# A two-layer hybrid inference step on one core: the instruction order of all engines found with a timeline model as the scheduler's clock

## The chip, the core and the metric

The kernel runs on one core of one Trainium2 chip. The metric is the device time of one launch in microseconds (us). Five engines work side by side, each on a queue of its own that it takes in order: PE (matrix products; PEld is its weight load, which overlaps), DVE and POOL (elementwise work), ACT (activations and copies) and SP (which here only issues DMAs). They wait for one another by semaphores that the framework places. All of the program is unrolled: one stream of instructions per engine, 34,294 in all, with no loop left at run time. So the order in each stream is fixed when the program is built, and it is what this change is about.

## What is computed

One step of a decoder trunk with two layers, for 528 prompt tokens (16 of them learned) and 8 sample sequences of 4 tokens, which carry states; 560 tokens of 1024 features in all. Cut to the frame:

```python
def _trunk(x, states, p, n_lead):
    for l in range(DEPTH):                     # DEPTH = 2
        if l % 2 == 0:
            mix, s_g, s_r, s_sh = _ab_mixer(...)   # GLA and RWKV-7 behind one input projection
        else:
            mix, c_buf, s_d = _c_mixer(...)        # gated DeltaNet, chunks, triangular solve
        x = _layer_norm(DEEPNORM_ALPHA * x + mix, ...)
        f, f_buf = _conv_ffn(x, ...)               # W_down(silu(conv3(x W_gate)) * (x W_up)), D_FF = 2816
        x = _layer_norm(DEEPNORM_ALPHA * x + f, ...)
```

All is float32 for the reader. The recurrences (RWKV-7, GLA, DeltaNet) carry a state per head from one tile of tokens to the next.

## The kernel before

**Products.** Each weight tile of 128 output features comes from memory as float32 (`wraw`, three buffers, fetched by SP at L117/118) and is split into a high part `wh` (ACT, L95) and a low part `wl` (DVE or POOL, L96). A product is three matmuls, high by high, high by low and low by high (`accum`, L145 to L150, the matmul at L148). One tile of a projection (`proj_h`, L157) is two halves of the tokens by eight tiles of 128 inputs by three, 48 matmuls, into a PSUM bank called `ph`.

**Layer 0** (`ab_layer`, L1772). First the RWKV projections that the first two pairs of heads need. Then core 0 (two pairs of heads: the recurrence) while the next projection tiles run beside it; what is then left of the projections; then core 1 (the other two pairs) while the GLA core runs beside it; then the output projection with residual and layer norm (`out_proj`), and the feed-forward block `ffn`, whose down projection ends in a layer norm as well. **Layer 1** (`c_layer`, L1836) is the same in kind: the inputs of four heads, core 0 beside the inputs of the other four, core 1 beside the gates and the finish of the first four, then output projection, norm, feed-forward and the last norm, which writes y.

**A core** goes through five tiles of tokens, the last of which holds the sample tokens. For each there is `prep` (L895 in RWKV, L1560 in DeltaNet): products of keys, a triangular inverse in up to six levels (`tri_inverse`, L684), a solve (`tri_solve`, L745). Then `step` (L976, L1656): the state's way through the tile, with the state update `pS` at L1009/L1010 (RWKV) and L1677 (DeltaNet). There are two sets of buffers, taken by the parity of the tile, so prep of tile i+2 waits for step of tile i. In an inverse level PE (`px`, `pt`, `pw`) and DVE (`X`, sums) take turns; nothing in one level can start before the one ahead of it is done. After the fifth tile the sample sequences' states are updated (`sample_states`, L1049 and L1717). The sample tokens' reads of their own states are `psr` (L272).

**What sets the order.** Python code traces all instructions, and each gets a priority from the place of its trace: a lower number goes first. The context (`tile.TileContext`, opened in `kernel` at L1921) holds a scheduler that goes through time with a clock: at each moment, each engine takes the instruction with the lowest number among those whose operands it holds to be ready. `beside` and `tick` (L166 to L178) hand the scheduler work to fill in with: at each tick of a core some pieces of a generator are traced, with their priority raised by an offset, so that they count as later work:

```python
    def tick(self):
        self.credit += self.rate
        while self.side is not None and self.credit >= 1:
            self.credit -= 1
            tc.cur_priority = tc.cur_priority + self.off
            if next(self.side, self) is self:
                self.side = None
            tc.cur_priority = tc.cur_priority - self.off
```

The rates are pieces per tick (.35 in core 0 of layer 0, .3 in both cores of layer 1, a piece being a half of a projection tile), the offsets 1000 and 1500. They are the same before and after the change. The projection tiles so handed over are called filler below; the `ph` matmuls are nearly all of it.

**The layer norm** (`LN`, L412 to L545) works by halves of the tokens of 280 and 280. A half's last projection comes in eight tiles by pairs (`pd`). After the second pair, a first estimate of the mean is made: DVE sums (L475, L478), a matmul `pc` (L479), a copy (ACT L483) and four subtractions of it on DVE (L487); then squares (ACT L500) and sums (POOL L489 to L495, DVE L490 to L517), a matmul pair `pst` (L520), the inverse deviation (L527 to L531), and the norm itself on eight tiles (DVE L539 multiplies, L540 subtracts, ACT L541 scales). The first half's norm runs beside the second half's projection. In the last norm each tile is then written to y (L543).

Of the kernel before, what the change touches and what calls it, by code (L numbers as in the profile page):

```python
# [48 lines left out]
class K:  # L49
# [26 lines left out]
    @contextmanager  # L76
    def later(self):
        """What is traced here gives way to what is traced after it."""
        tc = self.tc
        p = tc.cur_priority  # L80
        tc.cur_priority = p + 1000000
        yield
        tc.cur_priority = p
# [20 lines left out]
    def ahead(self, src, k):  # L104
        """The next projection's weights, prepared before what is traced until then."""
        self.pre.append(self.prepared(src, k))
# [14 lines left out]
    def proj_n(self, pool, src, xh, xl, cols, evict, room=None):  # L121
        """A projection to 32 outputs: the products with either part of the weights on 32 partitions each."""
        w, _ = self.prepared(src, KT, room) if room else self.weights(src, KT)
        for c, m in cols:
            ps = pool.tile([128, 512], F32, tag="pj", name="ph")
            for i in range(KT):
                for x in (xh, xl):
                    self.nc.tensor.matmul(
                        ps[:64, :m], w[:, i], x[:, i, c : c + m], start=(i == 0 and x is xh), stop=(i == KT - 1 and x is xl)
                    )  # L130
            evict(slice(c, c + m), ps[:64, :m])
            yield
# [24 lines left out]
    def proj_h(self, pool, src, k, xh, xl, cols, evict):  # L157
        """A projection by halves of the tokens, one PSUM bank each: evict(half, result)."""
        w = self.weights(src, k)
        for c, m in cols:  # L160
            ps = pool.tile([128, 512], F32, tag="pj", name="ph")
            self.accum(ps, w, k, xh, xl, c, m)
            evict(slice(c, c + m), ps[:, :m])
            yield

    def beside(self, gen, rate, off=OFF):  # L166
        """What gen traces is traced beside what follows, rate of its pieces at each tick."""
        self.side, self.rate, self.credit, self.off = gen, rate, 0.0, off
# [11 lines left out]
    def rest(self, off=0):  # L180
        """The end of what runs beside."""
        if self.side is not None:
            self.tc.cur_priority = self.tc.cur_priority + off
            for _ in self.side:
                pass
            self.tc.cur_priority = self.tc.cur_priority - off
        self.side = None

    def norm(self, bank, room, pieces, terms, eps, use):
        """1 / sqrt of sums over the features of four heads (weights, what is summed), a quarter of the partitions  # L190
        each, and from there, in two parts on two partitions, to all partitions: use(head, columns, result)."""
# [29 lines left out]
    def log_exp(self, after):  # L221
        """The table set with both functions, loaded when what gives them their input has been issued."""
        if self.table:
            return None
        self.table = True
        i = self.nc.scalar.preload_act_table_set("natural_log_exp_and_others")
        self.behind(i, after)
        return i
# [28 lines left out]
def room_for_reads(k, pool, **a):  # L257
    """Where the sample tokens of a sequence have columns of their own, among zeros: [sequence, kind and token]."""
    z = pool.tile([128, 576], F32, name="zq", **a)
    k.nc.gpsimd.memset(z, 0.0)  # L260
    return z


def sample_reads(k, z, xs, load, ps):
    """Two kinds of columns of the sample tokens times their own sequences' states."""
    for n, x in enumerate(xs):
        own = z[:, 32 * n : 32 * n + 544].rearrange("p (b w) -> p b w", w=68)[:, :, 0:4]
        k.nc.gpsimd.tensor_copy(own, x.rearrange("p (b c) -> p b c", c=4))
    for b in range(8):
        if b % 4 == 0:  # L270
            s = load(b // 4)
        k.nc.tensor.matmul(ps, z[:, 64 * b : 64 * b + 64], s[:, b % 4], start=(b == 0), stop=(b == 7))  # L272


def stack(k, x, a, quarters):
    """Both parts of x, of 32 tokens (partitions 96 to 128), on quarters of the partitions: with one factor as hlhl
    and the other as hhll, one pass has the products over the tokens with float32's accuracy."""
    nc = k.nc
# [8 lines left out]
class Tags:  # L287
    """A pool whose tags partly have a pool of their own."""
# [8 lines left out]
class Banks:  # L297
    """All of PSUM by pairs of banks, which are pools of their own: turn has those first that what was there before
    has left first. The first one (not used while kept is set) is where what comes after is to start."""
# [12 lines left out]
def weave(*gens):  # L312
    """The generators in turns."""
    gens = list(gens)
    while gens:
        for g in list(gens):
            if next(g, g) is g:
                gens.remove(g)
        yield
# [76 lines left out]
def out_proj(k, l, name, mixed, residual, pp):  # L396
    """Output projection of the mixer's features, residual and norm; what is left is x in r too."""
# [14 lines left out]
class LN:  # L412
    """Last projection into r, and layer norm over r's 1024 features, which lie on partitions and tiles; all by
    halves of the tokens, so that one half's norm runs beside the other's projection."""
# [87 lines left out]
    def stats(self, h, s):  # L502
        """Mean (in PSUM) and inverse deviation of a half of the tokens."""
# [44 lines left out]
def tiles(w):  # L548
    """[rows, columns] -> [column tile, partition, row tile, column]."""
    return w.reshape(-1, 128, w.shape[1] // 128, 128).transpose(2, 1, 0, 3)  # L550
# [39 lines left out]
def pack(i):  # L590
    """The arrays as the program reads them: layout alone."""
# [68 lines left out]
def pairs(b, L):  # L660
    """Blocks of 2b columns of which some are in the lower half."""
    return max(0, -(-(L - b) // (2 * b)))


def upper(ap, b, L):
    """Columns of the upper halves of those blocks."""
# [6 lines left out]
def lower(ap, b, L):  # L673
    """Columns of the lower halves: pieces of an AP."""
# [9 lines left out]
def tri_inverse(k, pool, pp, tag, lv, a, Wr, L, n):  # L684
    """(I + A)^-1 transposed, for n strictly lower A given transposed in a; lv: level masks (the first one as a
    is, the others transposed), so signed that what they leave of A is a part of -A. Entries of A, of the inverse
    and of what lies between are within [-1, 1] (products of contractions), and the solve refines what half
    precision leaves. Wr: room for the result."""
# [56 lines left out]
def tri_solve(k, pool, pp, tag, sub, W, ah, al, idr, R, L):  # L745
    """R = (I + A)^-1 R, one step of refinement with A in two parts (negated, as idr is, unless sub);
    R [tokens, part, head, column]."""
# [33 lines left out]
class RWKV:  # L781
    """RWKV-7 heads by pairs (128 features) and groups of two pairs."""
# [38 lines left out]
    def zrow(self, i, z):  # L821
        """One tile of the projection, mixed with the token before: columns in the order of tokens."""
# [16 lines left out]
    def pair(self, p):  # L839
        """Features of two heads: what the core reads."""  # L840
# [54 lines left out]
    def prep(self, prs, i):  # L895
        """What a tile of tokens needs before the state: U = G^T S + u0, with every solve done."""
# [63 lines left out]
    def read_states(self, prs):  # L960
        """The sample tokens times their own sequences' states: for R and for the outputs."""
# [14 lines left out]
    def step(self, prs, i, q, S):  # L976
        """The state's way through a tile, and the outputs."""
# [83 lines left out]
    def finish(self, g, c0, c1):  # L1061
        """Group norm, bonus and gate of some tokens, whose keys have given way to the outputs."""
# [55 lines left out]
class GLA:  # L1118
    """Gated linear attention: projections kept in DRAM until the core runs."""
# [22 lines left out]
    def decay(self, pj, stage, keep, xh, xl):  # L1142
        """The gates: their sums over tiles of tokens (b), and the factors of queries (e1) and keys (e2)."""
# [47 lines left out]
    def core(self, es, mx, side, oT):  # L1191
# [31 lines left out]
        def read(p):  # L1223
            """The sample tokens times their own sequences' states."""
# [113 lines left out]
    def finish(self, p1, prs, bank, o, c):  # L1338
        """Norm and gate of a half of the tokens, in place of what the core has read."""
# [24 lines left out]
class GDN:  # L1364
    """Gated delta net: heads by groups of four, each of 128 features."""
# [31 lines left out]
    def tokens(self):  # L1397
        """Decay and write strength, tokens on partitions."""
# [78 lines left out]
    def conv(self, c, out):  # L1477
        """One tile of q, k or v through the convolution and twice silu."""
# [81 lines left out]
    def prep(self, g, kq, i):  # L1560
        """What a tile of tokens needs before the state: U = G^T S + u0, with every solve done."""
# [71 lines left out]
    def spare(self, i, name, turn=0, dt=F32):  # L1633
        """Room: of its own, or of a tile's before."""
# [3 lines left out]
    def read_states(self, g, ks, qt, R, bank):  # L1638
        """The sample tokens times their own sequences' states: into R, and for the outputs."""
# [16 lines left out]
    def step(self, g, kq, i, q, S):  # L1656
        """The state's way through a tile, and the outputs."""
# [63 lines left out]
    def finish(self, g, c0, c1):  # L1721
        """Norm and gate; the scale that queries lack is left out of both sides of the norm but for its epsilon."""
# [172 lines left out]
def unpack(r):  # L1895
    """The device's arrays as the reference has them: layout alone."""
# [28 lines left out]
```

## Time and profile before

| | us |
|---|---|
| median of 3 runs | 1946.26 |
| the three runs | 1940.35, 1946.26, 1960.91 |
| span of the profiled execution, first to last instruction | 1932.2 |
| mean granted TensorE clock of that execution, as a share of full speed | 0.954 |

The page prints the span of the profiled execution, and not its whole time; what lies around the span is 8.1 us against the fastest of the three runs and 14.1 us against their median. Of a stretch of the span, PE's busy time, the number of its matmuls and the granted clock stand in one row; a matmul's own time in a row is longer than the distance to the next one, because they are pipelined, so the work of a stretch is best read as its length over its number of matmuls.

### The profile page before, as it was taken

What the parts mean: (1) busy time and instruction counts of PE and PEld (TensorE: products, weight loads), DVE (VectorE), ACT (ScalarE), POOL (GpSimd) and SP (SyncE); (2) the same over time, 40 slices, a digit from 0 to 9 for tenths busy, and PEclk for the clock granted to TensorE, in tenths of its full rate; (3) what the DMA queues carried; (4) which work ended last, traced back from release to release, by engine and by line L of the source; (5) the groups of instructions that cost most, each with busy time, mean ns of one, the idle gap of its engine ahead of it and who ended that gap; (6) DMA issues with size and microseconds to landing.
All of it is one profiled execution on the core that took longest, in us unless ns stands there. A gap on an engine that the chain in (4) does not pass through costs nothing.

```text
span 1932.2 us, 34294 instructions
## 1 busy us (share of the span) xinstructions
PE 1814.3 (94%) x13877; PEld 1689.1 (87%) x13877; DVE 1172.3 (61%) x2085; ACT 753.5 (39%) x1396; POOL 441.9 (23%) x705
## 2 busy tenths in 40 slices
PE   8999899899989999999979999899988999999995
PEld 8897788676889999999969997787778999999995
DVE  5766444555785535435776887687578653453457
ACT  6563324434353223213456454444344431232233
POOL 1323334222241000000141343332145200000001
PEclk9999999776899999999989999999889999999998
DMA  5110123211412222222322212412242122222231
GB/s 206 50 39 23 58 82 96 85 29 28 157 39 86 79 87 88 88 88 83 100 71 61 78 39 72 140 60 75 73 142 80 44 88 88 88 80 85 88 92 48
DMA packets 67358, 153.69 MB, mean 80 GB/s; under 512 B 15656, under 2 KB 26728, under 8 KB 67200
## 3 DMA queue, kind: packets, MB, share of 16 engines
q1 hardware_dynamic: 62784, 142.73, 24.1%
q10 hardware_dynamic: 3104, 4.15, 0.7%
q0 software_dynamic: 1312, 4.63, 0.6%
q8 instruction: 109, 1.79, 0.4%
q14 instruction: 49, 0.40, 0.1%
HBM read 136.72 MB, written 14.75 MB: 78 GB/s over the span
## 4 chain that ended last, share of the span: by engine, by line
PE 76%; DVE 11%; issue 3%; DMA 3%; ACT 3%; POOL 3%; SPq 0%; POOLq 0%; ACTq 0%; DVEq 0%
PE pd L148 14%; PE ph L148 13%; PE pg L148 13%; PE pu L148 13%; PE lead L148 2%; PE p L757 2%; PE pm L923 1%; PE psr L272 1%; PE pw L729 1%; PE px L713 1%; PE pt L723 1%; DVE r L487 1%; DMA wraw<-in_w_up 1%; PE psm L245 1%; DVE r L540 1%
## 5 line engine op out<-in xcount | busy, mean ns | idle before, releaser
L95 ACT CAST wh<-wraw 128x1024 fp32r<-128x1024 f32 x179 | 187.6, 1048 | 470.5 <-issue 164.0
L96 DVE TENSOR_TENSOR wl<-wraw,wh 128x1024 fp32r<-128x1024 f32 x158 | 193.7, 1226 | 206.3 <-ACT wh L95 206.2
L148 PE MATMUL ph<-xh,wh 128*128 128x280 f32 (+3 forms) x928 | 286.0, 309 | 16.5 <-ACT cp L1486 7.9
L148 PE MATMUL ph<-xh,wl 128*128 128x280 f32 (+3 forms) x928 | 283.9, 306 | 0.0
L148 PE MATMUL ph<-xl,wh 128*128 128x280 f32 (+3 forms) x928 | 283.6, 306 | 0.0
L148 PEld LDWEIGHTS ph<-xh,wh 128*128 128x128 f32 x928 | 179.4, 194 | 25.2 <-ACT cp L1486 8.1
L148 PE MATMUL pu<-xh,wl 128*128 128x264 f32 (+1 forms) x640 | 187.4, 293 | 0.0
L148 PE MATMUL pg<-xh,wl 128*128 128x264 f32 (+1 forms) x640 | 187.4, 293 | 0.0
L148 PE MATMUL pu<-xl,wh 128*128 128x264 f32 (+1 forms) x640 | 186.5, 291 | 0.0
L148 PE MATMUL pg<-xl,wh 128*128 128x264 f32 (+1 forms) x640 | 186.5, 291 | 0.0
L148 PE MATMUL pg<-xh,wh 128*128 128x264 f32 (+1 forms) x640 | 186.3, 291 | 0.0
L148 PE MATMUL pu<-xh,wh 128*128 128x264 f32 (+1 forms) x640 | 186.3, 291 | 0.0
L148 PEld LDWEIGHTS ph<-xh,wl 128*128 128x128 f32 x928 | 179.3, 193 | 5.1 <-issue 3.2
L148 PEld LDWEIGHTS ph<-xl,wh 128*128 128x128 f32 x928 | 179.2, 193 | 4.1 <-issue 2.9
L363 POOL COPY cn<-gp 128x2 f32<-128x2 f32 x44 | 31.2, 710 | 575.5 <-ACT gp L361 575.5
L148 PE MATMUL pd<-hl,wh 128*128 128x280 f32 x512 | 149.2, 292 | 0.1
L148 PE MATMUL pd<-hh,wl 128*128 128x280 f32 x512 | 149.2, 292 | 0.0
L148 PE MATMUL pd<-hh,wh 128*128 128x280 f32 x512 | 148.0, 290 | 0.0
L148 PEld LDWEIGHTS pu<-xh,wh 128*128 128x128 f32 x640 | 120.8, 189 | 0.0
L148 PEld LDWEIGHTS pg<-xh,wh 128*128 128x128 f32 x640 | 120.8, 189 | 0.0
L148 PEld LDWEIGHTS pg<-xl,wh 128*128 128x128 f32 x640 | 120.5, 188 | 0.0
L148 PEld LDWEIGHTS pu<-xh,wl 128*128 128x128 f32 x640 | 120.5, 188 | 0.0
(552 smaller groups left out, 4633.3 us busy)
## 6 DMA issues: line engine op xcount, KB each, us to landing
wraw<-in_w_up SPq DMA_DIRECT2D x88, 512.0 KB, 3.6
wraw<-in_w_down SPq DMA_DIRECT2D x32, 512.0 KB, 3.6
wraw<-in_w_c SPq DMA_DIRECT2D x32, 512.0 KB, 3.7
wraw<-in_w_ab SPq DMA_DIRECT2D x26, 512.0 KB, 3.6
wraw<-in_w_down SPq DMA_DIRECT2D x16, 384.0 KB, 3.5
wraw<-in_w_oab SPq DMA_DIRECT2D x8, 512.0 KB, 4.0
sb<-in_s_gdn SPq DMA_DIRECT2D x16, 256.0 KB, 2.7
so<-in_s_gdn SPq DMA_DIRECT2D x16, 256.0 KB, 3.3
```

The lines of the kernel that those rows point to most:

```text
L95: self.nc.scalar.copy(hi, src)
L96: (eng or self.nc.vector).tensor_sub(lo, src, hi.bitcast(F32))
L148: self.nc.tensor.matmul(ps[:, :m], a[:, i, :], x[:, i, c : c + m], start=(i == 0 and n == 0), stop=(i == k - 1 and n == 2))
L245: last = self.nc.tensor.matmul(ps[:, :m], lhsT, rhs[:, c : c + m], start=True, stop=True)
L272: k.nc.tensor.matmul(ps, z[:, 64 * b : 64 * b + 64], s[:, b % 4], start=(b == 0), stop=(b == 7))
L363: nc.gpsimd.tensor_copy(cn[:, f, 0, :], gp[:, 528:530])
L487: st(y, y, 1.0 if i < 4 else self.alpha, cb, op0=ALU.mult, op1=ALU.subtract)
L540: nc.vector.tensor_sub(t, t, mean)
L713: nc.tensor.matmul(up(px[:L, i]), a16[:L, i, :L], up(T[:L, i]), start=True, stop=True)
L723: nc.tensor.matmul(up(pt[:L, i]), W[:L, i, :L], up(X[:L, i]), start=not ta, stop=True)
L729: nc.tensor.matmul(pw[:L, i, :L], X[:L, i, :L], W[:L, i, :L], start=not wa, stop=True)
L757: nc.tensor.matmul(t[:L, i], a(h0 + i), x[:L, :, i], start=(j == 0), stop=(j == len(terms) - 1))
```

## The change

The context is opened with a flag: the scheduler's clock now comes from the framework's timeline model of the chip, in place of the one it has otherwise. What is traced, with which priorities, is the same; each instruction is in both programs. The other edits of the diff take docstrings away and put empty lines in their place, so that line numbers agree.

```diff
@@ kernel
-    with tile.TileContext(nc) as tc:
+    with tile.TileContext(nc, schedule_with_timeline_sim=True) as tc:
         trunk(tc, a, o)
```

What moves is the order on every engine (and with it which buffer of a set a tile gets, the semaphores, and ACT's table loads, 27 before and 29 now). Counted over the program of either order, the filler issued ahead of a state update, in projection tiles of 48 matmuls, stands like this; the first column is when that update ran in the profiled execution of before:

| state update | us, before | tiles ahead, before | tiles ahead, now |
|---|---|---|---|
| RWKV core 0, tiles 0 to 4 | 136.7, 165.1, 178.0, 207.7, 233.2 | 12.6, 14.4, 14.5, 15.7, 16.6 | 16.4, 17.0, 23.3, 23.3, 23.3 |
| RWKV core 0, sample states done | 249.2 | 17.5 | 24.3 |
| RWKV core 1, tiles 0 to 4 | 336.8 to 478.7 | 27.3 each | 27.3 each |
| DeltaNet core 0, tiles 0 to 4 | 1120.5, 1136.8, 1161.5, 1183.4, 1226.1 | 43.1, 44.0, 45.6, 46.7, 48.6 | 47.6, 48.2, 56.7, 56.7, 56.7 |
| DeltaNet core 1, tiles 0 to 4 | 1293.2, 1307.3, 1338.9, 1358.0, 1406.1 | 54.5, 55.1, 56.7, 56.7, 59.3 | 60.7 each |

The first place is PE in RWKV core 0, tile 4, around the reads of the sample states (`psr`); `ph` is filler, `p_2526` the solve, `pt` and `pw` a level of the inverse. Before:

```order
L272 MATMUL psr<-sb,zq 64x128 x8
L148 MATMUL ph<-xh,wh 128x280
L148 MATMUL ph<-xl,wh 128x280
L148 MATMUL ph<-xh,wl 128x280
L148 MATMUL ph<-xh,wh 128x280
L148 MATMUL ph<-xl,wh 128x280
L757 MATMUL p_2526<-sol_r,Wr 96x128 x4
```

Now, at the same reads (`pm` are products of keys, `pu` and `py` belong to the step):

```order
L912 MATMUL pt<-cst,vf 112x128
L912 MATMUL pt<-cst,ra 112x128
L272 MATMUL psr<-sb,zq 64x128 x8
L923 MATMUL pm<-ra,bn 128x256
L923 MATMUL pm<-ra,r 128x256
L989 MATMUL pu<-S,al 96x128 x2
```

No `ph` is left around the reads: all that may run beside this core stands ahead of them. DeltaNet's cores read alike at their `psr`.

The second place is PE in the second half of the last norm, around the estimate of the mean (`pc`); `pd` is the last down projection, of which 36 matmuls stand behind `pc` before the `pst` pair (the first five are shown). Before:

```order
L148 MATMUL pd<-hh,vl 128x280
L479 MATMUL pc<-lnc,cst 128x280
L148 MATMUL pd<-hh,vh 128x280
L148 MATMUL pd<-hl,vh 128x280
L148 MATMUL pd<-hh,vl 128x280
L148 MATMUL pd<-hh,vh 128x280
L148 MATMUL pd<-hl,vh 128x280
```

Now:

```order
L148 MATMUL pd<-hh,vl 128x280
L148 MATMUL pd<-hh,vh 128x280
L148 MATMUL pd<-hl,vh 128x280
L148 MATMUL pd<-hh,vl 128x280
L479 MATMUL pc<-lnc,cst 128x280
L520 MATMUL pst<-lnsum,cst 128x280
L520 MATMUL pst<-lnsq,cst 128x280
```

`pc` has gone behind all of `pd`. It has done so at the end of the first feed-forward block too; in the two output projections it went back by 15 and 21 `pd` matmuls.

The third place is DVE in the same stretch, where the first half's norm (L539, L540) and the estimate for the second half (L475, L478, L487) meet. Before:

```order
L472 SCALAR_TENSOR_TENSOR r<-r,pd 128x2x280
L540 TENSOR_TENSOR r<-r,lnc 128x280
L475 TENSOR_TENSOR lnc<-r 128x560
L540 TENSOR_TENSOR r<-r,lnc 128x280
L478 TENSOR_TENSOR lnc<-lnc 128x280
L539 TENSOR_TENSOR r<-r,lnsq 128x280 x2
L540 TENSOR_TENSOR r<-r,lnc 128x280 x2
L487 SCALAR_TENSOR_TENSOR r<-r,lnc 128x2x280 x4
```

Now:

```order
L531 TENSOR_TENSOR lnc<-pst,lnsq 128x280
L539 TENSOR_TENSOR r<-r,lnsq 128x280 x8
L475 TENSOR_TENSOR lnc<-r 128x560
L540 TENSOR_TENSOR r<-r,lnc 128x280 x8
L478 TENSOR_TENSOR lnc<-lnc 128x280
L487 SCALAR_TENSOR_TENSOR r<-r,lnc 128x2x280 x4
```

The eight tiles of the first half's norm, which before came by pairs of multiply and subtract, now come as eight multiplies and then eight subtracts, with the sums for `pc` among and behind them; the last norm has the same blocks of eight.

## Rows read from the trace of the kernel before

**Rows 1.** The page's first part: the span, and each engine's busy time.
```profile
span 1932.2 us, 34294 instructions
PE 1814.3 (94%) x13877; PEld 1689.1 (87%) x13877; DVE 1172.3 (61%) x2085; ACT 753.5 (39%) x1396; POOL 441.9 (23%) x705
```
**Rows 2.** Busy time (and instructions) of each engine by stretch, with granted clock.
```profile
core 0: us, PE busy (x) PEld busy (x) DVE busy (x) ACT busy (x) POOL busy (x), PEclk, DMA share, GB/s
...
61.90:178.00 116.10, 109.31 (x900) 95.42 (x900) 83.28 (x166) 55.04 (x115) 41.27 (x56) 1.00 0.12 38
178.00:249.20 71.20, 63.59 (x507) 51.90 (x506) 39.91 (x87) 26.24 (x59) 28.42 (x41) 0.98 0.18 54
249.20:336.80 87.60, 85.29 (x655) 76.22 (x654) 35.02 (x76) 29.49 (x53) 32.75 (x35) 1.00 0.29 84
336.80:496.10 159.30, 144.40 (x1008) 109.23 (x1008) 88.44 (x238) 70.64 (x185) 42.22 (x66) 0.71 0.18 53
...
564.10:945.00 380.90, 380.87 (x2951) 380.36 (x2950) 196.86 (x261) 116.75 (x173) 31.13 (x88) 1.00 0.30 89
...
1060.30:1161.50 101.20, 98.88 (x891) 95.22 (x891) 84.68 (x175) 50.91 (x97) 37.34 (x68) 1.00 0.18 56
1161.50:1226.10 64.60, 57.99 (x464) 48.84 (x463) 42.57 (x88) 28.25 (x52) 19.89 (x38) 0.97 0.21 66
...
1293.20:1406.10 112.90, 106.86 (x837) 88.70 (x836) 75.14 (x163) 46.64 (x86) 29.38 (x44) 0.94 0.22 68
...
1508.00:1884.60 376.60, 376.57 (x2917) 376.12 (x2916) 189.02 (x244) 110.24 (x161) 28.73 (x88) 1.00 0.28 84
```
**Rows 3.** The filler (ph) alone in those stretches: PE, PEld, DVE, ACT, clock.
```profile
61.90:178.00 116.10, 58.39 (x364) 49.36 (x363) 0.00 (x0) 12.84 (x33) 1.00 0.12 38
178.00:249.20 71.20, 27.73 (x144) 20.89 (x145) 0.00 (x0) 2.32 (x6) 0.98 0.18 54
249.20:336.80 87.60, 68.56 (x440) 59.62 (x439) 3.09 (x7) 7.06 (x18) 1.00 0.29 84
...
1060.30:1161.50 101.20, 67.41 (x432) 58.03 (x431) 0.00 (x0) 7.81 (x27) 1.00 0.18 56
1161.50:1226.10 64.60, 25.02 (x141) 20.52 (x141) 0.00 (x0) 2.51 (x9) 0.97 0.21 66
...
1293.20:1406.10 112.90, 38.57 (x232) 31.62 (x232) 4.39 (x10) 4.02 (x10) 0.94 0.22 68
```
**Rows 4.** Two stretches inside the cores 1, in which no filler stands.
```profile
465.10:499.20 34.10, 30.57 (x116) 22.04 (x115) 24.44 (x48) 16.78 (x40) 12.23 (x13) 0.50 0.19 57
1330.00:1377.00 47.00, 41.98 (x314) 30.52 (x314) 32.36 (x73) 19.48 (x36) 11.54 (x17) 0.85 0.24 70
```
**Rows 5.** An ACT group: line, operation, count, busy us, mean ns, idle before.
```profile
L232 ACT ACT_TABLE_LOAD x12 | 15.4, 1283 | 2.7 <-DVE ta L734 1.5 <-DVE ac L1500 1.1
```
**Rows 6.** PE's waits: what for, us in total, times, longest.
```profile
PE pst L520 <- DVE lnsum L517: 24.1, 8, 5.6
```
**Rows 7.** PE in the last norm: start, us, instruction, and idle time before it.
```profile
1895.23 0.71 PE L520 MATMUL pst<-lnsum,cst 128*128 128x280 f32 x2 [1.12 <-DVE lnsum L517]
...
1907.54 0.63 PE L479 MATMUL pc<-lnc,cst 128*128 128x280 f32 x2
...
1912.53 0.29 PE L148 MATMUL pd<-hh,vl 128*128 128x280 f32 x1
1917.93 1.27 PE L520 MATMUL pst<-lnsum,cst 128*128 128x280 f32 x2 [5.12 <-DVE lnsum L517]
```
**Rows 8.** DVE and ACT there, the same columns.
```profile
1908.63 3.90 DVE L487 SCALAR_TENSOR_TENSOR r<-r,lnc 128x560 f32<-128x560 f32 x4 [1.64 <-ACT lnc L483]
...
1918.18 0.45 DVE L517 TENSOR_TENSOR lnsq<-lnsq 128x280 f32<-128x280 f32 x1
...
1922.49 0.80 DVE L539 TENSOR_TENSOR r<-r,lnsq 128x280 f32<-128x280 f32 x2
...
1923.74 1.13 ACT L541 ACTIVATE r<-r,vec 128x280 f32<-128x280 f32 x2 [1.65 <-DVE r L540]
```

## The prediction

> **What bounds the kernel now.** I read the page's first part first [rows 1]: PE is busy 94% of the span, DVE 61%. So PE sets the time, and what can still be won or lost is where PE is idle or slow. Next I cut the span at the ends of the kernel's parts and read busy time, matmuls and clock by stretch [rows 2]. The feed-forward block of layer 0 gives the price of a matmul with nothing in its way: 380.90 us for 2951, that is 129 ns, at clock 1.00. The order there is the same in both programs, and so it is in the second block (376.60); these 757 us can't change. Then I asked for the filler alone [rows 3]. At 129 ns a filler matmul, the rest of a stretch is what the recurrence's own matmuls (the chain) cost, holes included:
>
> - RWKV core 0 up to tile 2: 116.10 less 364 x 0.129 leaves 69.1 us for 536 chain matmuls, 129 ns each.
> - RWKV core 0 from there to its end: 71.20 less 18.6 leaves 52.6 for 363, 145 ns.
> - the rest of the projections: 87.60 less 56.8 leaves 30.8 for 215, 143 ns.
> - DeltaNet core 0 up to tile 2: 45.5 for 459, 99 ns; from there to tile 4, 64.60 less 18.2 leaves 46.4 for 323, 144 ns.
> - DeltaNet core 1: 112.90 less 29.9 leaves 83.0 for 605, 137 ns.
> - RWKV core 1 beside GLA, without filler: 159.30 for 1008, 158 ns, with the clock at 0.71.
>
> The more filler there is per chain matmul, the less a chain matmul costs, since the waits of the inverse's levels are covered: 0.94 per chain matmul goes with 99 ns, 0.4 with 137 to 145. Where none is left, a chain alone costs 47.00 us for 314, 150 ns, at clock 0.85 [rows 4].
>
> **The change, part by part.** Nothing is added or removed but order. The two added table loads on ACT cost 1.28 us each [rows 5]; ACT is busy 39% and gets them beside PE, so 0, or +2.6 if both fall into a chain.
>
> *Filler comes early.* By the table of the change, 23.3 tiles stand ahead of RWKV's tile 2 update where 14.5 did: 8.8 tiles, 422 matmuls, 54.5 us of work that moves forward and is as long there as where it came from. What changes is the price of the chain beside it. Up to tile 2 there are now 786 filler matmuls for 536 chain ones. The floor is DeltaNet's 99 ns: 536 x 30 ns = 16 us won. The ceiling is no gain, as PE's idle time there is only 6.8 us [rows 2] and the rest is matmuls that are slow in themselves. I take 110 ns, between that idle time and the floor: **-10**. DeltaNet's first stretch is at 99 ns already: **0**. The weights come along: 8.8 tiles of 512 KB in a stretch with a DMA share of 0.12 [rows 2], and the splits on ACT (55.04 of 116.10 busy) and POOL (41.27); these covers hold, and if SP's queue kept a state's load behind a weight fetch, the chain would wait for some us.
>
> *The holes.* In return the chain goes alone from tile 2 on. At the price of the nearest stretch without filler: RWKV 363 x (158 - 145) = +4.7; DeltaNet core 0 323 x (150 - 144) = +2.1; DeltaNet core 1, 605 x (150 - 137) = +7.8. Together **+14.6**. From below these are 0 (the chain costs what it does now); from above, a hole stays as long as it was with its filler, that is 18.6 + 18.2 + 29.9 = +66.7. I take the first because the 47 us without filler are of this very chain. The projections that are left between the cores then have 114 filler matmuls where they had 440; 215 x 7 ns is **+1.5**.
>
> *RWKV core 1 beside GLA.* No filler in either order, only another mix of two chains. Below: the 143 ns of the stretch ahead of it, -15. Above: its own worst part, 34.10 us for 116 matmuls or 294 ns at clock 0.50 [rows 4], met by as many again, 116 x 136 ns = +16. I take **0**.
>
> *The norms.* PE waits 24.1 us for the sums in front of `pst`, at eight places [rows 6]. Four are first halves, like the 1.12 us of [rows 7], where eight to ten more `pd` matmuls (1.0 to 1.3 us) now stand ahead: **-4**. Four are second halves, 5.12 in the last norm. There `pc` now stands behind 36 `pd` matmuls. `pc` ran at 1907.54 and the last `pd` at 1912.53; from the copy of `pc` on, DVE is nearly without a gap from 1908.63 to 1918.6 [rows 8], so a later `pc` moves all of it: 36 x 0.129 = 4.6. DVE's new order (eight multiplies ahead of the first subtract) also lets ACT start its last eight scalings some 2.2 us later (from 1923.74 in [rows 8]); it needs 4 x 1.13 = 4.5 us for them, which puts y's end about 1.2 later. **+5.8** at the end of the kernel, **+4.5** at the end of the first feed-forward block, which has the same shift. In the output projections `pc` goes back 21 and 15 matmuls (2.7 and 1.9 us), part of which the next projection's matmuls cover: **+1**. If that cover and DVE's gaps took it all, this whole part would be -4 and not +7.3.
>
> **Sum:** -10 + 14.6 + 1.5 + 0 - 4 + 5.8 + 4.5 + 1 = +13.4 us on a span of 1932.2. What lies around the span isn't printed; the profiled execution stands 14.1 below the median of the runs shown, and I set the difference on that median: 1946.3 + 13 = **1959 us**, 0.7% more.
>
> **Rivals.**
>
> *Faster: filler is used better.* A chain that is served at once in the filled stretches (99 ns, -16) reaches tile 2 sooner, the holes cost what their chain does now (0), and the two chains in core 1 are mixed to 143 ns (-15); with the norms' +7 that is -24: 1922. For it: 6.8 and 14.9 us of PE's idle time in those two stretches [rows 2] lie open to a better clock. Against it: in DeltaNet, where most of the holes are, the filled stretch has only 2.3 us of idle time left to win.
>
> *Slower: the holes are bound by latency, and lose the clock.* In a hole the time is that of PE, DVE and PE in turn, and taking filler out gives little back. If half of the filler's 66.7 us comes back, the holes cost 33 in place of 14.6 and the sum is +32, 1978; if none does, +65, 2011. It decides from where the holes lose over 21 us. For it: the granted clock was 0.71 over the 159 us without filler, and 0.50, the lower of its two levels, 1.2 of 2.4 GHz, in a part where PE ran 116 matmuls in 34 us [rows 2, 4]; with filler it was 1.00. Against it: 0.85 and 150 ns in DeltaNet's 47 us. The Trainium skill, "TensorE: Matmul & The Clock Gate", section "HAM oscillation — how this bites in real kernels", says that matmuls in bursts with waits between them fall back to half the clock again and again. This trace agrees (0.71 against 1.00). By that rule each hole would go towards the 294 ns a matmul of the 34 us, and this rival would be the likelier; by the 47 us of [rows 4] it is not.
>
> *A mere exchange.* Holes and remaining projections at the prices that they have now, the first filled stretch -10, the norms +7: -3, 1943. It is what follows if filler time is just additive wherever it stands.
>
> **How the numbers follow.** A measurement of this kernel can tell about 1%, 19 us, from no change. Chances: forecast 0.34, faster 0.27, slower by latency 0.27, exchange 0.12. Of the forecast 0.25 lies within 1%, 0.07 above (the core 1 term's +16 is enough), 0.02 below; of the faster rival 0.24 beyond 1% and 0.03 within; of the exchange 0.10 within and 0.02 below. So faster 0.28, same 0.38, slower 0.34. The range takes in the faster rival's 1922 and a little under it, and the slower one past its half-way case up to 2000; the forecast's own range, by the bounds of core 1 beside GLA, is 1944 to 1975.
>
> **What would show it.** In the changed kernel: the stretch up to RWKV's tile 2 some 44 us longer with clock 1.00 and about 110 ns a chain matmul; from tile 2 on no `ph`, 150 to 158 ns a matmul and a clock under 0.9; `pst` of the last norm about 5 us after the last `pd` as before, but with `pc` and the four L487 in between, so about 10. I am wrong if DeltaNet's core 1 takes under 83 us without filler (then the chain wasn't slowed) or over 100 (then it is latency), if RWKV core 1 beside GLA moves by more than 15 us either way, or if the feed-forward blocks differ from 380.9 us at all.

## The result, and the profile after

The changed kernel takes 2044.41 us (median of 4 runs, 2036.27 to 2046.89) against 1949.01 of the kernel before: a ratio of 1.054, with a 95% interval of 1.048 to 1.060. It is slower by 5.4%; the prediction had 1959 and a range up to 2000. The profiled execution of the changed kernel took 2042.98, with a span of 2041.0, so 2 us lie around a span; the profile of before (1932.2) is thus of an execution somewhat quicker than the median, and the two spans differ by 108.8.

The page's first part, which answers to [rows 1], and its line of granted clocks by slices of 51 us:

```profile
span 2041.0 us, 34233 instructions
PE 1869.1 (92%) x13877; PEld 1745.4 (86%) x13877; DVE 1167.8 (57%) x2085; ACT 750.7 (37%) x1398; POOL 430.1 (21%) x705
...
PEclk9999868577899999999889999588768999999997
```

The work is the same, and DVE's, ACT's and POOL's busy time has hardly moved. PE's busy time rose by 54.8 us for the same 13,877 matmuls, while its share of the span fell from 94 to 92%. The mean clock fell from 0.954 to 0.903, and the slices where it fell most are those of the two layers' recurrences.

The stretches of [rows 2] have other ends now. These are cut at the same state updates (tile 2 of RWKV core 0, its sample states, tile 0 of core 1, the end of core 1; the first feed-forward block; then from the end of layer 0's last norm, which is 1018.70 in the kernel before, to tile 2 of DeltaNet core 0, to its tile 4, its sample states, and tile 0 to 4 of DeltaNet core 1). Columns as in [rows 2]:

```profile
61.90:239.20 177.30, 175.23 (x1393) 160.10 (x1393) 95.03 (x185) 76.37 (x150) 64.79 (x81) 0.97 0.22 66
239.20:317.20 78.00, 66.21 (x372) 50.62 (x372) 40.38 (x92) 27.46 (x61) 19.13 (x33) 0.71 0.05 12
317.20:359.40 42.20, 35.60 (x293) 33.66 (x292) 24.24 (x61) 16.56 (x39) 21.45 (x32) 0.85 0.49 158
359.40:535.30 175.90, 161.69 (x1089) 129.08 (x1088) 98.90 (x255) 66.41 (x167) 35.25 (x54) 0.69 0.15 44
...
586.00:966.00 380.00, 376.73 (x2914) 375.85 (x2914) 196.44 (x261) 116.72 (x173) 28.39 (x88) 1.00 0.29 89
...
1044.00:1264.20 220.20, 216.53 (x1787) 207.92 (x1787) 164.19 (x316) 116.50 (x220) 63.79 (x121) 0.98 0.23 71
1264.20:1326.40 62.20, 44.10 (x264) 35.96 (x264) 22.58 (x48) 13.90 (x25) 13.93 (x25) 0.67 0.18 55
1326.40:1351.50 25.10, 17.79 (x87) 11.18 (x86) 19.66 (x36) 7.96 (x13) 9.24 (x9) 0.83 0.61 191
...
1396.20:1514.60 118.40, 86.73 (x572) 70.72 (x571) 58.59 (x138) 34.10 (x66) 27.03 (x42) 0.72 0.08 25
```

And the filler in them, as [rows 3]:

```profile
61.90:239.20 177.30, 116.18 (x758) 101.46 (x758) 0.00 (x0) 18.86 (x48) 0.97 0.22 66
239.20:317.20 78.00, 8.85 (x48) 8.50 (x48) 0.39 (x1) 0.40 (x1) 0.71 0.05 12
...
1264.20:1326.40 62.20, 0.00 (x0) 0.00 (x0) 0.00 (x0) 0.00 (x0) 0.67 0.18 55
...
1396.20:1514.60 118.40, 0.00 (x0) 0.00 (x0) 0.00 (x0) 0.00 (x0) 0.72 0.08 25
```

Read the last pairs against [rows 2, 3]. From tile 2 to tile 4 of DeltaNet core 0 there were 141 filler matmuls, 18.2 us of PE; now there are none, and the stretch takes 62.20 us where it took 64.60. From tile 0 to tile 4 of core 1 there were 232, 29.9 us; now none, and it takes 118.40 where it took 112.90. A chain matmul in these stretches costs 236 and 207 ns now (62.20 over 264, 118.40 over 572), not 150. On balance, the filler that stood there had cost nothing. The pairs are not quite alike: 59 and 33 chain matmuls have moved ahead of these stretches as well (323 before and 264 now, 605 and 572), so the price per matmul is too high as a comparison, and the length is what counts. Two runs below compare stretches with the same chain in them.

What the chain of waits says of tile 4 of DeltaNet core 0 in the changed kernel (start, us, what; `psr` are the reads of the sample states, `sb` their loads, two buffers for eight of them; `p` is the solve, `pu` and `pS` the step):

```profile
1266.02 3.52 DMA Gr<-rows
...
1288.99 3.38 PE psr L272 x16
1292.38 3.08 DMA sb<-in_s_gdn
...
1295.51 1.98 PE psr L272 x8
1297.51 3.94 DMA sb<-in_s_gdn
...
1301.50 1.98 PE psr L272 x8
1303.50 2.88 DMA sb<-in_s_gdn
...
1311.11 1.66 PE p L757 x6
...
1322.28 1.84 PE pu L1670 x8
...
1324.97 1.65 PE pS L1677 x8
```

and in the kernel before:

```profile
1193.35 1.03 PE psr L272 x8
1194.40 2.83 DMA sb<-in_s_gdn
...
1197.37 1.06 PE psr L272 x8
...
1205.41 2.83 DMA sb<-in_s_gdn
...
1218.65 0.94 PE p L757 x6
...
1223.31 1.08 PE pu L1670 x8
...
1225.35 0.98 PE pS L1677 x8
```

It is one row of steps, each after the last: load, eight reads, load, eight reads, then the solve and the step. What is slower in it now are PE's own steps: eight reads take up to 1.98 us in place of 1.03, six matmuls of the solve 1.66 in place of 0.94, the step's `pS` 1.65 in place of 0.98. The clock was 0.63 from 1289 to 1307 and 0.56 from there to the end. Added up over the reads, the solve's two runs of six, `pu` and `pS`, that is about 6 us of the 62.20, an estimate from these rows. So the stretch is a length of waits with a lower clock on top of it, and filler there did two things: it took PE time, and it kept the clock up.

In whole, by state updates, the 108.8 us come so. The rows of before, cut at the same matmul as those of the changed kernel (0.7 and 0.5 us behind the cuts of [rows 2] at 178.00 and 336.80):

```profile
61.90:178.70 116.80, 110.01 (x911) 96.11 (x910) 83.45 (x167) 55.04 (x115) 41.29 (x57) 1.00 0.12 38
178.70:249.20 70.50, 62.89 (x496) 51.20 (x496) 39.74 (x87) 26.24 (x59) 28.40 (x41) 0.98 0.18 54
249.20:337.30 88.10, 85.79 (x661) 76.72 (x660) 35.16 (x76) 29.99 (x54) 33.17 (x36) 1.00 0.29 85
...
1018.70:1161.50 142.80, 139.44 (x1184) 132.50 (x1183) 112.51 (x235) 76.33 (x149) 43.73 (x88) 0.99 0.20 60
```

The stretches ahead of the two tile 2 updates grew by 60.5 and 77.4, the projections between the cores shrank by 45.9 and 4.1: that is filler moved forward (394 matmuls or 50.8 us in layer 0, 11 tiles or 68 us in layer 1). The recurrences that it left (from tile 2 on in the cores 0, core 1 of layer 1, all with their sample states) did not shrink, but grew by 19.6. The rest, 1.3 in sum, is RWKV core 1, which grew by 17, the output projections, which shrank, and the norms.

### The profile page after: what moved, and what is told of

It is laid out like the page before. It is cut to its first block, busy times and chain, and to the rows that moved or that the text cites. A ratio compares the mean times of both kernels' runs of the same rounds, so it can differ in the third digit from the quotient of the medians.

```text
span 2041.0 us, 34233 instructions
## 1 busy us (share of the span) xinstructions
PE 1869.1 (92%) x13877; PEld 1745.4 (86%) x13877; DVE 1167.8 (57%) x2085; ACT 750.7 (37%) x1398; POOL 430.1 (21%) x705
## 4 chain that ended last, share of the span: by engine, by line
PE 78%; DVE 9%; ACT 5%; DMA 5%; issue 2%; POOL 0%; ACTq 0%; SPq 0%; DVEq 0%; POOLq 0%
PE ph L148 16%; PE pd L148 16%; PE pg L148 12%; PE pu L148 12%; PE p L757 3%; PE pm L923 2%; PE lead L148 2%; PE pw L729 1%; PE psr L272 1%; PE px L713 1%; PE pt L723 1%; DMA sb<-in_s_gdn 1%; DVE vl L96 1%; DVE r L539 1%; DMA Gr<-rows 1%
## 5 line engine op out<-in xcount | busy, mean ns | idle before, releaser
L148 PE MATMUL ph<-xl,wh 128*128 128x280 f32 (+3 forms) x928 | 279.4, 301 | 0.0
L148 PE MATMUL ph<-xh,wl 128*128 128x280 f32 (+3 forms) x928 | 279.1, 301 | 0.0
```

The lines of the kernel that those rows point to most:

```text
L148: self.nc.tensor.matmul(ps[:, :m], a[:, i, :], x[:, i, c : c + m], start=(i == 0 and n == 0), stop=(i == k - 1 and n == 2))
```

## The experiments

Theory A says that the filler's place is the cause, theory B that the timeline clock orders the chain itself badly. Within A, A1 blames the lower clock in the stretches without filler, A2 the latency of the chain, which filler doesn't lengthen. Medians of the kernel before beside these runs lay between 1942 and 1944 us.

**Filler early, with the old clock.** The rates are raised and the offsets lowered:

```diff
-CFG = {... 'R0': 0.35, ... 'O0': 1000, ... 'R2': 0.3, 'R3': 0.3, 'O2': 1500, 'O3': 1500, ...}
+CFG = {... 'R0': 0.7, ... 'O0': 300, ... 'R2': 0.8, 'R3': 1, 'O2': 200, 'O3': 0, ...}
```

Expected: 

> The kernel before, with its own scheduler clock, and the filler asked for earlier: rates .7, .8, 1 and offsets 300, 200, 0. By its order 15.6, 19.5, 22.0, 22.1, 22.7 tiles stand ahead of the state updates of RWKV core 0, and in DeltaNet core 1 all of it. Theory A (place of the filler): 2015 to 2060 us, with chain matmuls at 200 ns or more in the stretches without filler and clock 0.65 to 0.75 there. Theory B (fine order): within 1% of 1949, since the order inside the chain is the old scheduler's.

Measured: 2051.96 us, 1.060 times before [1.051, 1.068]. From tile 0 to tile 4 of DeltaNet core 1 no filler stood, and the row reads like that of the changed kernel:

```profile
1397.40:1521.20 123.80, 90.36 (x637) 72.77 (x636) 65.84 (x155) 35.84 (x70) 29.66 (x46) 0.73 0.09 28
```

That is 194 ns a matmul. So the old clock, too, makes this kernel slow when it is asked to put the filler early. Theory A.

**All filler ahead of its core, under either clock.** Three lines trace what would run beside a core before it (the scheduler may still let some of it slip into the core):

```diff
+            k.rest()
             rw.core(0)
...
+        k.rest()
         gd.core(0)
...
+        k.rest()
         gd.core(1, fe)
```

Old clock, expected: 

> The kernel before, with its own clock, and all filler traced ahead of the core that it ran beside, so that the recurrences run alone. Theory A2 (a core takes its latency with or without filler, so filler outside it costs its full time): the filler of the cores, some 33 tiles less the ones that stood outside already, about 20 tiles or 125 us, comes back as length: 2050 to 2110. Additive filler: 1945 to 1985.

New clock, expected: 

> The changed kernel with the same edit. The filler's place is then nearly the same under both clocks. If the place of the filler is all that made the changed kernel slow, this one is within 20 us of its partner with the old clock. If the timeline clock's order inside the chain is worse in itself, it is slower by over 30 us; if it is better, faster by over 20.

Measured: 2088.57 [1.065, 1.082] with the old clock, 2083.77 [1.066, 1.079] with the new one. With the filler in nearly the same place the two clocks differ by 5 us, which these intervals, each some 15 us either way, don't tell from nothing. So theory B can't carry the loss of 95 us: in sum, the new clock's order of the chain is neither better nor worse by more than some 20. It isn't the same in every part: DeltaNet's core 1, without filler in either, takes 116.60 us by the old order and 126.50 by the new one, which other stretches give back. In the old clock's run, DeltaNet's core 0 (tile 0 to 4) and core 1 have these rows; under them the filler in the first:

```profile
1277.50:1381.10 103.60, 86.23 (x701) 75.87 (x700) 57.09 (x135) 33.80 (x64) 30.11 (x46) 0.88 0.17 52
1453.90:1570.50 116.60, 86.46 (x592) 70.17 (x592) 60.19 (x143) 35.15 (x67) 27.89 (x43) 0.72 0.08 26
...
1277.50:1381.10 103.60, 24.31 (x134) 18.83 (x134) 2.61 (x6) 2.39 (x6) 0.88 0.17 52
```

The kernel before takes 105.6 us for that core 0 (1120.5 to 1226.1) with 261 filler matmuls; here it takes 103.6 with 134 (additive filler: 16.4 less), and with nearly the same chain in it (579 and 567 matmuls). The new clock's row for core 1:

```profile
1421.90:1548.40 126.50, 93.56 (x580) 76.69 (x580) 61.28 (x141) 34.54 (x67) 26.98 (x42) 0.66 0.08 24
```

**The same work cut out of both.** The last four gate projections are left out:

```diff
...
+            if g:
+                nc.vector.memset(z[:, 0:NT], 1.0)
+                yield
+                yield
+                continue
```

From the kernel before, expected: 

> The kernel before without the last four gate projections of layer 1 (192 filler matmuls, 24.8 us at 129 ns; the output gate of those four heads is then a constant). Most of them stand between tile 3 and tile 4 of DeltaNet core 1. Theory A2 (filler in a latency-bound stretch is free): the time falls by 0 to 9 us. Additive filler: it falls by 20 to 28 us.

From the changed kernel, expected: 

> The changed kernel without the same four projections. There all of them stand ahead of core 1's first state update, where PE is full. Both theories: 20 to 30 us off 2044; what tells is the difference to the same cut in the kernel before: near 0 by additive filler, 15 to 25 us by theory A2.

Measured: 1929.64 and 2021.31. The changed kernel loses 23.1 us against 2044.41, as 192 matmuls at 129 ns are worth (24.8). The kernel before loses 13.4 of 1943.04 (ratio 0.994, interval 0.990 to 0.998, so 4 to 19 us), more than theory A2's 9 and less than the 20 of additive filler: by its time alone this run doesn't decide. Its trace does, for the stretch in question:

```profile
1290.70:1404.70 114.00, 94.89 (x708) 74.84 (x708) 73.07 (x162) 41.88 (x78) 28.93 (x45) 0.87 0.19 58
...
1290.70:1404.70 114.00, 18.14 (x104) 14.40 (x104) 2.16 (x5) 2.00 (x5) 0.87 0.19 58
```

Core 1 from tile 0 to tile 4, 104 filler matmuls in place of 232, takes 114.00 us in place of 112.90, with the same chain (604 and 605 matmuls); additive filler would have taken 16.5 off. On balance the 128 that left had been free; the clock fell from 0.94 to 0.87 without them. (The other 64 stood behind it.)

The changed kernel's run with the cut has a second use. From tile 2 to tile 4 of DeltaNet core 0, PE's instructions are the same in the same order as in the changed kernel, and the clock was 0.74 in place of 0.67:

```profile
1263.20:1321.40 58.20, 41.18 (x265) 33.54 (x263) 22.65 (x49) 13.88 (x25) 13.73 (x23) 0.74 0.18 56
```

That is 4.0 us less for the same order, of which some 2.4 are loads that landed sooner and the rest PE's steps at the higher clock. So a difference of 4 us in one stretch of two executions proves nothing by itself. One level of the inverse ran at a clock of 1.00 here and of 0.53 there: 1.73 us against 1.87. So an inverse level hardly depends on the clock, and what the clock costs, it costs in the reads, the solve and the step.

**The latency itself.** If the length of these stretches is a row of steps, taking a step out of the row must shorten them with all the work kept. Two switches trace the sample tokens' reads ahead of tile 4's inverse:

```diff
-CFG = {... 'GS': 0, ... 'RS': 0, ...}
+CFG = {... 'GS': 1, ... 'RS': 1, ...}
```

In the changed kernel, expected: 

> The changed kernel with the sample tokens' reads of their states (psr, with their loads) traced ahead of tile 4's inverse instead of behind it, in all cores (switches GS and RS at 1). The filler's place by the order is the same. Theory A2 (a hole is the latency of one tile's chain, in which three of the state loads and the reads stand in a row behind the inverse): the stretches from tile 2 to tile 4 of DeltaNet's two cores lose 8 to 20 us each, in all 15 to 35 us off 2044. Theory A1 (a hole is PE work at half clock): the work is the same, so within 8 us of 2044.

In the kernel before, expected: 

> The kernel before with the same two switches, as a control: its tile 2 to tile 4 stretches have filler in them, and by theory A2 they too are a chain's latency, so they shorten as well where PE has room, by up to 10 us each, total 1915 to 1950. If filler and chain simply add (the prediction's way), nothing moves: 1935 to 1950.

Measured: 2010.98 in the changed kernel, 33 us less (1.034 of before, against 1.054) and within the 15 to 35 expected of A2, and 1933.08 in the kernel before, ratio 0.994 [0.990, 0.998]. In the changed kernel the two stretches lose 12.6 and 9.0:

```profile
1260.70:1310.30 49.60, 37.44 (x264) 29.99 (x263) 22.65 (x48) 13.46 (x25) 13.53 (x24) 0.79 0.22 68
1379.70:1489.10 109.40, 85.11 (x571) 70.45 (x571) 58.38 (x138) 34.10 (x66) 27.07 (x42) 0.73 0.09 27
```

The number of matmuls is that of the changed kernel (264, and 571 for 572), and still they are done 12.6 and 9.0 us sooner, more than the 4 us by which one order differed between executions: theory A2. Of the kernel before, DeltaNet's core 1 gains while RWKV's core 0 loses 6 us (60.7 for 54.7), which led to the next run.

**The switch for DeltaNet alone, in the kernel before.**

```diff
-CFG = {... 'GS': 0, ...}
+CFG = {... 'GS': 1, ...}
```

Expected: 

> The kernel before with the reads ahead of the inverse in DeltaNet alone (switch GS at 1). In the run with both switches DeltaNet core 1 took 98.4 us from tile 0 to tile 4 in place of 112.9, and RWKV core 0 took 60.7 from tile 2 to tile 4 in place of 54.7. If these two belong to the two switches, this one keeps the gain without the loss: 1920 to 1932, clear of the 1943 of before. If the 14 us were the chance of one execution, 1938 to 1948.

Measured: 1921.18 us, ratio 0.990 [0.985, 0.995]: quicker than both kernels of this study. Core 1 from tile 0 to tile 4, 112.90 before, with 161 of its 232 filler matmuls still in it:

```profile
1297.90:1398.30 100.40, 94.29 (x763) 78.93 (x762) 68.88 (x154) 42.78 (x80) 28.00 (x43) 0.93 0.22 66
```

With the reads early and no filler, the changed kernel took 109.40 us for this core at a clock of 0.73 (above). There the filler did not only cost nothing: the stretch with it was the shorter one. How much of these 9 us is the clock and how much the order of the chain was not separated.

**The clock in the stretches without filler.** Matmuls of no use keep PE at work while the inverse waits (four ahead of each `px` and `pw`), and in a second try two there and sixteen ahead of each four state reads:

```diff
         px = ps("px")
+        for _ in range(k.warm):
+            nc.tensor.matmul(px[:L, :, :L], a16[:L, 0, :L], a16[:L, :, :L], start=True, stop=True)
...
```

First try, expected: 

> The changed kernel, with four matmuls that are of no use ahead of each px and each pw of the inverse, in tiles 3 and 4 of the cores 0 and in all of DeltaNet core 1: 432 of 448 columns, into the bank that the px or pw behind them overwrites, while PE waits there. The results stay the same. Theory A1 (the holes are long because the clock falls to its lower level): the clock in the holes rises over 0.9 and the three holes lose 40 us or more, 2005 or less. Theory A2 (they are long by latency, PE and DVE in turn): the clock rises but the time is 2035 to 2080, as the added matmuls only fill waits or lengthen them.

Second try, expected: 

> The changed kernel with idle matmuls that fit the waits: two ahead of each px and pw (0.43 us in a wait of about 0.45) and sixteen ahead of each four reads of the sample states (2.1 us in a load's wait of about 3), tiles 3 and 4 of the cores 0 and DeltaNet core 1. The four of the earlier try lengthened a level from 1.84 to 2.9 us. If the lower clock has a share in the holes, the clock there rises over 0.85, psr and solve go at full speed and the stretches tile 2 to 4 of core 0 and tile 0 to 4 of core 1 lose 5 to 15 us together, total 2025 to 2040. If the holes are waits alone, 2040 to 2055.

Measured: 2069.79 and 2081.27, both slower than the changed kernel. In the first the clock in tile 2 to 4 of RWKV core 0 rose from 0.71 to 0.83, with the length as it was (78.00):

```profile
239.30:318.00 78.70, 69.63 (x427) 50.23 (x426) 41.74 (x92) 27.71 (x61) 18.94 (x31) 0.83 0.10 31
```

In DeltaNet's cores the clock rose as well (0.67 to 0.85, 0.72 to 0.82) and the stretches grew by 4.6 and 10.1:

```profile
1270.00:1336.80 66.80, 49.43 (x330) 37.68 (x329) 24.65 (x51) 14.99 (x27) 15.47 (x24) 0.85 0.17 52
...
1419.80:1548.30 128.50, 102.38 (x713) 79.00 (x712) 60.00 (x139) 34.84 (x66) 27.99 (x42) 0.82 0.09 27
```

The added matmuls stand in PE's queue, 0.86 us ahead of each `px` and `pw`, and were longer than the waits (a level of the inverse in tile 4 went from 1.84 to 2.9 us). They also raised the clock in the wrong place: in the inverse, where it hardly matters, and not in the solve behind it, where it was 0.60 from 1320 to 1337. The second try missed both of its ranges. It kept the clock at 1.00 over the reads of tile 4 in DeltaNet core 0. But the sixteen are 32 matmuls in the trace, and take 3.4 us in place of the 2.1 expected; with them the reads became a full PE row of 32.7 us where they had taken 18.6:

```profile
1299.50:1332.20 32.70, 31.12 (x321) 30.23 (x320) 0.43 (x1) 0.00 (x0) 2.48 (x8) 1.00 0.18 58
```

A higher clock bought with work in the chain didn't give back the loss, and the run with the reads moved, whose work is the same, did shorten the stretches, so A1 is not the main cause. How much of the whole loss the lower clock carries stays open, since neither try raised it without lengthening the chain; the estimate for one stretch is the 6 us of 62.20 above.

**Holding the filler back under the new clock.** Each filler tile's split waits for a small copy from the chain, and the rates are lowered to .2 and .15:

```diff
+            self.nc.scalar.copy(mk[0:1], self.at)
...
+            self.nc.scalar.copy(wh[0:1, 0, 0:1], mk[0:1])
```

Expected: 

> The changed kernel, with the filler tied to the chain: a small ACT copy from the chain's latest tile stands ahead of each filler tile's weight split, so a filler tile cannot start before that point of the recurrence, and the rates are lowered to .2 and .15. By its order the state updates then have 11.0, 12.1, 14.0, 15.0, 17.0 tiles ahead in RWKV core 0 and 42.2 to 46.3 in DeltaNet core 0, near to what before has. Theory A (where the filler stands is the cause): 1935 to 1970 us, holes at 137 to 150 ns a chain matmul, clock over 0.94. Theory B (the timeline clock's fine order of the chain itself is worse): over 2010 us, whatever the filler does.

Measured: 2068.23, a miss. By its number it is what theory B was to give (over 2010), and the runs above speak against B; by theory A it should have been fast. Up to tile 2 of RWKV core 0 it has only 337 filler matmuls, yet:

```profile
61.90:222.30 160.40, 134.59 (x934) 119.84 (x934) 82.93 (x181) 60.72 (x128) 33.94 (x56) 0.78 0.06 21
```

That is 196 ns a chain matmul (160.40 less 337 x 0.129, over 597), with 26 us of PE idle and the clock at 0.78. The reason may lie in how many filler matmuls are put in one place. Counted in the programs, between two `px` of a DeltaNet or RWKV core 0 inverse stand 0 to 21 filler matmuls by the old clock's order and 18 to 51 by the new one's, as long as there is filler; in the trace a level then mostly takes 1.9 to 3.6 us by the old order and 5.5 to 8 by the new one, and 1.8 to 2.2 with none. The waits of a level have room for about eight (1.84 us less two runs of 0.39 on PE is 1.06, over 0.129). So the new clock fills them two to six times over; tied to the chain, the filler came in lumps, 17 to 25 matmuls in one or two levels of an inverse and few or none in the others. That this density is what makes the tied kernel slow was argued from these counts, and not tried by itself; nor were the added copies, which stand in ACT's queue between the chain's own. How the filler is spread under the new clock is thus an open end of theory A.

## Why the prediction was wrong, by its steps

- **The step that failed is the holes' term, +14.6.** It priced a chain matmul without filler at 150 to 158 ns, from one stretch of 47 us [rows 4] and the two mixed chains of core 1, and so had 52 of the 66.7 us of filler come back. Measured, a chain matmul there costs 207 to 236 ns and nothing came back: 64.60 to 62.20, 112.90 to 118.40, and 70.50 to 78.00 with 96 filler matmuls fewer. The 47 us were the densest part of core 1: 314 of its 605 chain matmuls, with the steps of two tiles (updates at 1338.9 and 1358.0) beside the preparation of the next. Where one tile's chain goes alone its matmuls are few, and its time is set by the row of steps. The fall of cost per chain matmul with filler beside it, which the prediction took for cover of waits, fits this too: a fixed length, divided by the chain's own matmuls after taking off filler that had been free. Its own sign for this came: core 1 of DeltaNet took over 100 us without filler.
- **The rival "bound by latency" was the true case**, by its kind and its point of decision. Its ceiling, +65 or 2011, was too low by 33: it left out the filler beside the sample states and behind core 1 (73 and 64 matmuls, 18 us), and the 20 us by which these recurrences grew, in sum all of it in the sample states (15.8 to 26.4 us in RWKV core 0, 18.3 to 25.1 and 19.8 to 22.0 in DeltaNet's cores; the clock there was 0.50 to 0.83, against 0.88 to 1.00 before). Why they grew was not followed up; in part other work of the chain now runs inside them. It also held the -10 of the next point, which did not come. I set it behind the forecast because of the 47 us.
- **The gain in the filled stretch, -10, did not come.** 177.30 us for 758 filler and 635 chain matmuls is 125 ns a chain matmul against 129: PE was already full there in the kernel before, so more filler only added its own length.
- **The clock** behaved as forecast in direction: 0.67 to 0.72 in the stretches without filler, 0.97 to 0.98 ahead of them. That matmuls in bursts between waits fall back to half clock, as the Trainium skill says ("TensorE: Matmul & The Clock Gate", section "HAM oscillation — how this bites in real kernels"), this trace bears out; but the clock is the smaller part of what holds these stretches: about 6 us of 62.20 by the estimate above, and half clock or full made 1.87 or 1.73 us of an inverse level.
- **RWKV core 1 beside GLA, 0:** right only together with what follows. 159.30 became 175.90, which is more than the 15 us that the prediction named as a sign of being wrong; but 81 matmuls of what follows run inside it, and the output projection behind it is shorter by 17.
- **The norms, +7.3:** about right in sum. From the start of its feed-forward block, the end of layer 0's last norm comes 4.2 us later (412.0 to 416.2) and the end of the kernel 3.4 (408.2 to 411.5); the first halves' waits are nearly gone. `pc` now stands behind all of `pd`, and the `pst` behind it waits for what 1912.53 to 1917.93 showed before [rows 7]:

```profile
2015.35 0.63 PE L479 MATMUL pc<-lnc,cst 128*128 128x280 f32 x2
2025.79 1.27 PE L520 MATMUL pst<-lnsum,cst 128*128 128x280 f32 x2 [9.81 <-DVE lnsum L517]
```

- **The feed-forward blocks** did not move (380.90 and 380.00 for stretches of nearly the same matmuls).

## What to carry to other kernels

Ask of a stretch with filler in it how long it would be without: when the answer is "as long", the filler there is free on balance, and an order that moves it to where PE is full pays its whole price there. A price per matmul, got by taking filler off a stretch and dividing, hides just this; the row of steps in the chain of waits, with its loads and turns between engines, shows it. The new order used up the filler where PE was full anyway, so compare two orders by place and by lump (how many filler matmuls between two steps of the chain) and not by total; and the best gain here, 1%, came from taking the reads and their loads out of the row, not from the scheduler.

## What was not expected

Filling waits with useless matmuls cost 25 to 37 us although it raised the clock (0.67 to 0.85 in one stretch): the four ahead of a `px` took 0.86 us, and the step behind them began that much later when the wait was shorter. And with the filler in nearly one place, two schedulers whose orders differ in nearly every row came within 5 us of each other (2088.57 and 2083.77).
